# Spreading an mLSTM's running maxima by a DRAM round trip instead of matmuls, and the last layer norms in three VectorE steps: one change to a streaming encoder layer

## The chip, the cores and the metric

The kernel runs on one core of one Trainium2 chip. The metric is device time in microseconds for one execution of the whole layer; a figure for a kernel is the median of its runs. One execution was also recorded by the hardware profiler; its own time and its span (first to last instruction) are given beside the runs, since the views of the profile belong to that execution.

The core's engines each run their own instruction stream: PE (TensorE, with its weight loads listed apart as PEld), DVE (VectorE), ACT (ScalarE), POOL (GpSimd) and SP (SyncE, which only issues transfers here). DMA transfers are issued from an engine's queue and run beside the engines; SPq and POOLq are the queues of SP and GpSimd.

## The reference, cut to what matters

One layer of an encoder is computed for a prompt of 2048 tokens and a batch of 8 short samples of 16 tokens, model width 1024. Two groups of heads work on one input projection; their outputs are concatenated, projected, added to the input and normalised; a convolutional feed-forward block with its own norm follows.

```python
def trunk_layer(x, ...):
    qm, km, vm, om, ip, fp, qa, ka, va = split_in(x @ w_in)
    logi, logf = ip + b_igate, log_sigmoid(fp + b_fgate)
    hm, C1, n1, m1 = mlstm_chunkwise(qm, km * 128**-0.5, vm, logi, logf, C0, n0, m0)
    hm = sigmoid(om) * head_norm(hm, g_mlstm_norm)
    ha = sliding_window_attention(rope(qa), rope(ka), va)
    h = layer_norm(ALPHA * x + concat(hm, ha) @ w_out, ln1_g, ln1_b)
    f = conv_ffn(h, conv_prev, w_up, w_conv, b_conv, w_down)
    return layer_norm(ALPHA * h + f, ln2_g, ln2_b)

def layer_norm(x, g, b):
    return (x - mean(x)) * rsqrt(var(x) + 1e-5) * g + b
```

The mLSTM has 4 heads of 128. It goes through the prompt in chunks and carries a matrix memory `C`, a vector `n` and a stabiliser `m` per head:

```python
    def step(carry, inp):
        C, n, m = carry
        qc, kc, vc, li, lf = inp
        b = cumsum(lf)
        inter = b + m
        dmat = where(causal, b[:, None] - b[None, :] + li[None, :], -inf)
        mt = maximum(inter, max(dmat))
        w_inter = exp(inter - mt)
        s = (qc @ kc.T) * exp(dmat - mt[:, None])
        num = w_inter * (qc @ C) + s @ vc
        den = w_inter * (qc @ n) + sum(s)
        h = num / maximum(abs(den), exp(-mt))
        ...
```

Write `M` for the running maximum of `li - b` and the carried `m`, so that `mt = b + M`. Then `w_inter = exp(m - M)`, and the weight of source position s for query position l is `exp(li - b at s, minus M at l)`. The kernel works with `M` directly: it needs `M` of each query position along the free axis of a tile, the same on all 128 partitions.

## The kernel before

**Tiling.** Tokens come in 17 tiles of 128: 16 of the prompt (`NPT`) and one that holds the 8 x 16 sample tokens. The mLSTM takes a whole prompt tile of 128 as one chunk. All products of weights with tokens are done with three matmuls, each operand split in a high and a low part: `split` (L215) has ScalarE cast the high part (L217) and VectorE subtract it from the source (L218). Dense projections use a Strassen-like scheme of seven products per block.

**Stages.** By the trace: input projection until about 650 us (`i_product`, L688), output projection until about 890 (`group` and `o_block`, matmuls at L222 to L224, with the first norm, `norm`, L1548), a transition, up-projection from 935 to 1880 (matmuls at L1831), and down-projection until the end (`f_downs`, matmuls at L2034).

**How the recurrent work is woven in.** `Chains` (L157) holds three generators: the sample tile, the mLSTM of the prompt (`m_chain`, L1039) and the windowed attention (`a_chain`). While the input and output projections run, each dense piece of work adds its cost in ns to a clock, and a generator takes its next step once its due time has passed and enough of the five PSUM banks of the chains are expected to be free. A step says at its `yield` what it cost, after how long the next one is due and how many banks that one needs. These numbers only set the order in which instructions are written. TensorE keeps exactly that order (its schedule is manual, L230 and on); the instructions of the other engines are ordered by the framework's scheduler, each engine then runs its own list in order.

**One prompt tile of the mLSTM before.** `m_rows` (L1065) transposes the gates into rows of four heads by 128 positions, scans the cumulative sum `bc`, forms `a_` = li - b and scans the running maximum `M` (L1072), starting from the carry `self.mc`. `hilo` (L1004) splits `M` into two fp32r parts, `hl`. `y_row` writes -b - M into the rows 32 to 35 of `ay`, whose rows 0 to 3 hold `a_`. The next carry is b + M at the last position (L1076).

`m_tile` (L1175) then spreads `M` over the partitions on TensorE: `m_rep` (L1090) multiplies `hl` with a selector, one matmul per head, into the PSUM bank `pm`, which then holds -M on all partitions. `m_cols` (L1013) multiplies the broadcast carry with an identity (plain fp32, which appears as two matmuls) and transposes `ay`, both into `pcol`, and copies 40 columns to SBUF. VectorE adds the causal mask, giving `dt` (L1099); ScalarE makes `emt`, then four steps `wi` = exp(pm + carry) (L1111) and four steps exp(dt + a) (L1105). Next come the scores `qk @ k` and the transposed keys on TensorE, and VectorE's products `sd`, `kw` and `qk * wi` (L1192). Last come `pnum` (L1199 and the line behind it), which takes `sd` and the weighted `qk`, and the new memory `C`. In a tile's rhythm the load and `m_rows` of the next tile are written after the head norm of this one.

Two lines carry the spreading:

```python
self.nc.tensor.matmul(pm[:, h], self.sel[:, h:h + 1].to_broadcast([36, P]), self.hl[i], start=True, stop=True)
nc.tensor.matmul(ps[:, 0:4], mp.to_broadcast([MH, P]), self.ident[:MH, :MH], start=True, stop=True)
```

**GpSimd's other work in these stages** is a memset of the ones column of `v1` in `m_load` (L1079), and in each norm the power -1/2 of variance + eps, `lsc` (L1545), on one column.

**The down-projection.** `f_downs` goes through three blocks of tiles (`FBLOCKS`, 6, 6 and 5), in each through seven products and in each product through six units of the inner dimension. After the last unit of a product, `after` (L2037) empties its banks: for product 1 ScalarE copies one bank to another, the tile `fht` (L2041), which the matmuls of a later product go on adding to; for the others VectorE adds the bank to the sum `yacc` of a token tile. When a tile's sum is complete, `finish` (L2065) is appended to `pending`; in each unit the first two entries of `pending` advance by one step. `finish` runs `norm_steps` (L1561): the first step takes the statistics; the second computes -mean times `lsc` on VectorE (one column), the normalised tile on ScalarE (L1567), the product with g on VectorE (L1568) and the addition of b on GpSimd (L1569; on VectorE in the last block), and issues the transfer of the result from GpSimd's queue (from SP's in the last block). The last tiles of the last block go through `norm_last`, on VectorE and SP alone. `d_weights` (L1952) and `d_tokens` (L1970) run five and six units ahead: SP issues the weight load `wraw`, then `split` makes `uw` from it and `fu` from the tokens `r`.

Of the kernel before, what the change touches and what calls it, by code (L numbers as in the profile page):

```python
# [8 lines left out]
F32 = mybir.dt.float32  # L9
# [5 lines left out]
P = 128  # L15
# [8 lines left out]
MH = 4  # L24
# [180 lines left out]
class Prog:  # L205
# [89 lines left out]
    def setup(self):  # L295
# [14 lines left out]
        self.zw = [dp.tile([4, P, 1024], F32, name=f"zw{j}") for j in range(NFF)]  # L310
        self.zc = [dp.tile([P, 2, len(FBLOCKS[0]) * P], F32, name=f"zc{j}") for j in range(NFF)]
        self.zt = dp.tile([2, NK2, P, D], F32, name="zt")
        self.zf = [dp.tile([NFF, P, len(b) * P], F32, name=f"zf{i}") for i, b in enumerate(FBLOCKS)]
# [613 lines left out]
    def t_setup(self):  # L927
# [31 lines left out]
        nc.vector.memset(self.C, 0.0)  # L959
        self.mc = self.one("mc0", [MH, 1])  # L960
        nc.vector.memset(self.mc, 0.0)
# [32 lines left out]
    def row(self, nm, dt=F32):  # L994
        return self.work("r_" + nm, [MH, P], dt, 1 if nm == "b" else 2)

# [15 lines left out]

    def m_cols(self, i, mp=None):  # L1013

        nc = self.nc
        ps = self.bank([P, 40], "pcol")
        if mp is not None:
            nc.tensor.matmul(ps[:, 0:4], mp.to_broadcast([MH, P]), self.ident[:MH, :MH], start=True, stop=True)
        nc.tensor.transpose(ps[:, 4:40], self.ay[i], self.ident[:36, :36])
        c0 = 4 if mp is None else 0  # L1020
        col = self.work("col", [P, 40], bufs=2)
        nc.vector.tensor_copy(col[:, c0:], ps[:, c0:])
        return col

    def m_emt(self, col):
        emt = self.work("emt", [P, MH], bufs=2)
        self.nc.scalar.activation(emt, col[:, 36:40], AF.Exp)
        return emt
# [10 lines left out]
    def m_chain(self):  # L1039
# [4 lines left out]
        for t in range(NPT):  # L1044
# [3 lines left out]
            if pend is None:  # L1048
                pend = self.m_load(t, b, ti), *self.m_rows(t, b, ti)
                yield 300, 7000, 2  # L1050
            else:
                yield 0, 1000, 2
            hn = self.m_norm(*(yield from self.m_tile(t, *pend)))
# [11 lines left out]
    def m_rows(self, t, b, ti):  # L1065
        V = self.nc.vector
        lf, li = self.gate_rows(self.logs_of(b), ti)
        i = t % 2
        bc, a_, M = self.row("b"), self.ay[i][0:4], self.row("M")
        V.tensor_tensor_scan(bc, lf, self.seg[:, 0], 0.0, op0=ALU.add, op1=ALU.add)  # L1070
        V.tensor_sub(a_, li, bc)
        V.tensor_tensor_scan(M, self.seg[:, 0], a_, self.mc, op0=ALU.add, op1=ALU.max)  # L1072
        self.hilo(i, M)
        self.y_row(i, bc, M)
        mp, self.mc = self.mc, self.work("mc", [MH, 1], bufs=3)
        V.tensor_add(self.mc, bc[:, P - 1:P], M[:, P - 1:P])  # L1076
        return i, mp

# [17 lines left out]

    def m_masked(self, pm, mask):
        dt = self.work("dt", [P, MH, P])
        self.nc.vector.tensor_tensor(dt, pm, mask.rearrange("p (o m) -> p o m", o=1).to_broadcast([P, MH, P]), op=ALU.add)  # L1099
        return dt  # L1100

    def m_exps(self, dt, col):

        for h in range(MH):
            self.nc.scalar.activation(dt[:, h], dt[:, h], AF.Exp, bias=col[:, 4 + h:5 + h])  # L1105

    def m_inter(self, pm, col):

        wi = self.work("wi", [P, MH, P])
        for h in range(MH):  # L1110
            self.nc.scalar.activation(wi[:, h], pm[:, h], AF.Exp, bias=col[:, h:h + 1])  # L1111
        return wi

# [60 lines left out]

    def m_tile(self, t, load, i, mp):  # L1175
        nc = self.nc
        V = nc.vector
        qk, v1, og = load
        pm = self.m_rep(i)
        col = self.m_cols(i, mp)  # L1180
        dt = self.m_masked(pm, self.mcau)
        yield 600, 2800
        emt = self.m_emt(col)
        wi = self.m_inter(pm, col)
        self.m_exps(dt, col)
# [162 lines left out]
    def t_sample(self):  # L1348
# [8 lines left out]
        lf, li = self.gate_rows(self.logs_of(b), ti)  # L1357
        bc, M = [self.row(n) for n in ("b", "M")]
        ar = self.work("sd", [MH, P], name="ar")
# [8 lines left out]
        nc.sync.dma_start(a["m_s"], ms)  # L1368
        x = self.work("dt", [MH, P], name="x")

# [177 lines left out]
    def norm(self, y, g, bb, z):  # L1548
# [10 lines left out]
        self.nc.sync.dma_start(z, y)  # L1559

    def norm_steps(self, y, g, bb, adder=None):  # L1561
        nc = self.nc
        V = nc.vector
        mv, s = self.stats(y)
        yield
        V.scalar_tensor_tensor(s[:, 1:2], mv[:, 0:1], -1.0, s[:, 0:1], op0=ALU.mult, op1=ALU.mult)
        nc.scalar.activation(y, y, AF.Identity, bias=s[:, 1:2], scale=s[:, 0:1])  # L1567
        V.tensor_mul(y, y, g)  # L1568
        (adder or nc.gpsimd).tensor_add(y, y, bb)  # L1569

# [428 lines left out]
    def f_downs(self):  # L1999
# [65 lines left out]
        def finish(t, b, step):  # L2065
            if b == nb - 1 and step == 3:
                self.norm_last(ys[t], *ln2, a["y"][t], st if t == last_tile else None)
                return
            end = b == nb - 1
            yield from self.norm_steps(ys[t], *ln2, V if end else nc.gpsimd)  # L2070
            (nc.sync if end else nc.gpsimd).dma_start(a["y"][t], ys[t])

# [55 lines left out]
```

## Time and profile before

| | us |
|---|---|
| median of 3 runs | 2362.39 (2361.93 to 2363.34) |
| the profiled execution, its own time | 2366.53 |
| its span | 2364.8, granted TensorE clock 0.994 |

Busy time by stage in that execution, from a view of busy time in windows of the span:

| stage (us) | PE | DVE | ACT | POOL | DMA share | GB/s |
|---|---|---|---|---|---|---|
| 0 to 300, input projection | 287.6 | 210.7 | 133.7 | 15.0 | 0.83 | 286 |
| 300 to 650, input projection | 344.6 | 268.6 | 244.5 | 12.0 | 0.90 | 304 |
| 650 to 890, output projection | 240.0 | 202.7 | 149.5 | 24.8 | 0.69 | 231 |
| 935 to 1880, up-projection | 934.1 | 722.1 | 516.1 | 90.9 | 0.83 | 284 |
| 1880 to 2365, down-projection | 466.8 | 391.5 | 219.5 | 61.0 | 0.61 | 202 |

How the rows of the trace read. A row of the timeline gives the start in us from the span's start, the duration in us, the engine, the line of the kernel (L1072 is line 1072), the operation, out<-in by tile names with their shapes, and how many instructions are joined in it; brackets at its end give the engine's idle time ahead of it and what ended that. A row of the windows gives the stretch, its length, then busy time (and instructions) of PE, PEld, DVE, ACT and POOL, the granted clock (1.00 is full speed), the mean busy share of the 16 DMA engines, and GB/s. A row of the waits names an engine, the group that waited, the engine and tile that released it, and then total us, number and mean. A row of the DMA issues gives out<-in, the queue, how many, the size of each and the median us from issue to landing. A row of the groups gives after its count the total busy us and the mean ns of one, then the idle time ahead of it and what ended most of it.

### The profile page before, as it was taken

Reading aid. Unit: us, or ns where it says so; the run is one execution under the profiler, and the core shown is the slowest. Engines: PE = TensorE matmul, PEld = TensorE weight load, DVE = VectorE, ACT = ScalarE, POOL = GpSimd, SP = SyncE. Lnnn points to the kernel's source line nnn. Section 1 sums busy time; section 2 is a strip of 40 time slices with the busy share of each in tenths; the row PEclk is TensorE's granted clock in tenths of the full one; section 3 lists DMA queues with packets and bytes.
Section 4 is the critical chain, followed back from the end, with each engine's and each line's share of the span. In section 5 each row is a group of like instructions: output and inputs, shape, how many; then the busy total and the mean of one; then the engine's idle time right before and its main releaser. Section 6 shows DMA issues by size and latency. Waiting matters only on the chain.

```text
span 2364.8 us, 39830 instructions
## 1 busy us (share of the span) xinstructions
PE 2316.2 (98%) x14425; PEld 2122.7 (90%) x14425; DVE 1834.5 (78%) x3221; ACT 1284.3 (54%) x2423; POOL 209.4 (9%) x281
## 2 busy tenths in 40 slices
PE   8999999999999999999999999999999999999998
PEld 7999999899987777999999999999999978778776
DVE  8676587797688888987888676777766786895987
ACT  5453366777766565555556455555544544544543
POOL 0001000000000112200000000002000100400400
PEclk9999999999999999999999999999999999999999
DMA  7888889889976657887777889878988776657653
GB/s 279 283 302 286 288 287 324 276 291 318 314 264 227 225 204 248 286 306 289 274 270 257 307 316 314 308 242 297 315 275 260 212 284 219 232 170 219 228 166 107
DMA packets 296933, 624.98 MB, mean 264 GB/s; under 512 B 47004, under 2 KB 140192, under 8 KB 296736
## 3 DMA queue, kind: packets, MB, share of 16 engines
q1 hardware_dynamic: 294144, 612.99, 76.3%
q0 software_dynamic: 1728, 6.29, 0.7%
q10 hardware_dynamic: 864, 3.15, 0.3%
q8 instruction: 114, 1.87, 0.3%
q14 instruction: 83, 0.68, 0.1%
HBM read 451.78 MB, written 170.56 MB: 263 GB/s over the span
## 4 chain that ended last, share of the span: by engine, by line
PE 69%; DVE 7%; DMA 3%; issue 2%; ACT 1%; POOL 1%; SPq 0%; DVEq 0%; POOLq 0%; ACTq 0%
PE dps L1831 18%; PE fup L1831 18%; PE fht L2034 5%; PE dps L700 5%; PE dps L2034 5%; PE fup L2034 3%; PE dps L222 2%; PE dps L224 2%; PE dps L223 2%; PE ppo L1337 1%; DVE uw L218 1%; PE ppt L1331 1%; PE psc L1288 1%; DVE hl L218 1%; DMA yacc<-zh 1%
## 5 line engine op out<-in xcount | busy, mean ns | idle before, releaser
L1831 PE MATMUL dps<-hh,uw 128*128 128x384 f32 (+1 forms) x1848 | 481.5, 329 | 6.7 <-ACT u L1856 1.9
L1831 PE MATMUL fup<-hh,uw 128*128 128x384 f32 (+1 forms) x1848 | 480.1, 328 | 2.5 <-ACT u L1856 2.1
L1831 PEld LDWEIGHTS dps<-hh,uw 128*128 128x128 f32 x1848 | 330.0, 188 | 10.3 <-ACT u L1856 2.9
L1879 DVE SCALAR_TENSOR_TENSOR cc<-u,cw,cc 128x768 f32<-128x768 f32 (+1 forms) x264 | 252.4, 977 | 106.2 <-ACT cc L1877 104.3
L1831 PEld LDWEIGHTS fup<-hh,uw 128*128 128x128 f32 x1848 | 330.1, 188 | 3.6 <-ACT u L1856 2.9
L1831 PE MATMUL fup<-hl,uw 128*128 128x384 f32 (+1 forms) x924 | 302.9, 328 | 1.7 <-DVE hl L218 1.7
L1831 PE MATMUL dps<-hl,uw 128*128 128x384 f32 (+1 forms) x924 | 302.5, 327 | 0.0
L700 PE MATMUL dps<-w,oh 128*128 128x256 f32 x1344 | 258.7, 287 | 2.6 <-DVE zev L773 1.1
L217 ACT CAST w<-wraw 128x1024 fp32r<-128x1024 f32 (+2 forms) x167 | 163.0, 984 | 141.4 <-PE dps L700 67.8
L218 DVE TENSOR_TENSOR w<-wraw,w 128x1024 fp32r<-128x1024 f32 (+2 forms) x167 | 189.1, 1139 | 56.2 <-ACT w L217 53.6
L217 ACT CAST uw<-wraw 128x1024 fp32r<-128x1024 f32 x126 | 122.9, 978 | 196.8 <-PE dps L2034 99.3
L700 PEld LDWEIGHTS dps<-w,oh 128*128 128x128 f32 x1344 | 213.4, 190 | 14.6 <-issue 8.9
L218 DVE TENSOR_TENSOR uw<-wraw,uw 128x1024 fp32r<-128x1024 f32 x126 | 150.7, 1198 | 63.4 <-ACT uw L217 63.1
L1877 ACT ACTIVATE cc<-u,cw 128x768 f32<-128x768 f32 (+1 forms) x132 | 129.6, 997 | 118.0 <-DVE u L1870 60.2
L700 PE MATMUL dps<-w,ol 128*128 128x256 f32 x672 | 189.2, 282 | 0.0
L2034 PE MATMUL fup<-uw,fu 128*128 128x512 f32 x726 | 178.2, 401 | 9.5 <-ACT fht L2041 6.9
L2034 PEld LDWEIGHTS fup<-uw,fu 128*128 128x128 f32 x726 | 138.1, 191 | 45.0 <-ACT fht L2041 7.8
L700 PE MATMUL dps<-oh,w 128*128 128x256 f32 x896 | 167.1, 282 | 10.0 <-ACT zev L759 3.7
L1831 PEld LDWEIGHTS fup<-hl,uw 128*128 128x128 f32 x924 | 173.5, 188 | 2.5 <-DVE hl L218 2.5
L1831 PEld LDWEIGHTS dps<-hl,uw 128*128 128x128 f32 x924 | 173.5, 188 | 0.0
L2034 PE MATMUL dps<-uw,fu 128*128 128x512 f32 x660 | 165.0, 395 | 0.0
L700 PEld LDWEIGHTS dps<-oh,w 128*128 128x128 f32 x896 | 139.7, 188 | 16.1 <-issue 4.1
(326 smaller groups left out, 4596.2 us busy)
## 6 DMA issues: line engine op xcount, KB each, us to landing
uw<-zw SPq DMA_DIRECT2D x176, 512.0 KB, 4.6
zw<-uw SPq DMA_DIRECT2D x88, 512.0 KB, 3.1
w<-zws SPq DMA_DIRECT2D x72, 512.0 KB, 6.3
wv<-wup SPq DMA_DIRECT2D x66, 512.0 KB, 5.5
wraw<-wi SPq DMA_DIRECT2D x65, 512.0 KB, 4.7
wraw<-zt SPq DMA_DIRECT2D x60, 512.0 KB, 4.2
wraw<-wdn SPq DMA_DIRECT2D x45, 512.0 KB, 4.1
wraw<-wo SPq DMA_DIRECT2D x40, 512.0 KB, 4.6
```

The lines of the kernel that those rows point to most:

```text
L217: nc.scalar.copy(hi, src)
L218: nc.vector.tensor_sub(lo, src, hi.bitcast(F32))
L222: mm(out, ah, bh, start=start, stop=False)
L223: mm(out, ah, bl, start=False, stop=False)
L224: mm(out, al, bh, start=False, stop=stop)
L700: mm(o, l, r, start=s in (1, 7) and c == k == i == 0, stop=k == 3 and i == 2, skip_group_check=True)
L1288: nc.tensor.matmul(ps[kvh][:, j, :nk], q[rs, j0 + j], k[rs, sel], start=i == 0, stop=i == 2)
L1331: nc.tensor.transpose(pp[:, j * P:(j + 1) * P], scs[j // 2][:, 2 * kvh + j % 2, kt * P:(kt + 1) * P], self.ident)
L1831: mm(ps, l[:, k], r[:, k], start=s in (1, 7) and k == 0 and i == 0, stop=k == 3 and i == 2, skip_group_check=True)
L1877: S.activation(c[:, v], u[:, v, 2:2 + n], AF.Identity, bias=w[3], scale=w[2])
L1879: V.scalar_tensor_tensor(c[:, v], u[:, v, i:i + n], w[i], c[:, v], op0=ALU.mult, op1=ALU.add)
L2034: mm(ps, l[:, k, c], r[:, k], start=s in (1, 4, 7) and u == 0 and k == 0 and i == 0, stop=u == nu - 1 and k == n - 1 and i == 2, skip_grou ...
```

## The change

Two parts that do not touch each other.

**The maxima.** The tile of `M` becomes four rows of 129: 128 maxima and, in the last column, the carry the scan starts from. `m_rows` no longer splits it. It issues, on GpSimd's queue, a transfer of these rows to a small DRAM tile `zM` (two of them, used in turn), and behind it, on the same queue, a transfer that reads the 516 numbers back to every one of 128 partitions, into the SBUF tile `wi` (one buffer). The read waits for the write to land. `m_cols` keeps only the transpose of `ay`; `m_rep` is called for the sample tile alone. `dt` is now the mask minus `wi`, read from SBUF; `m_inter` overwrites `wi` in place with exp(-wi + its last column). The next carry is written into the last column of the next tile's rows. The costs and banks that `m_chain` and `m_tile` declare are lowered to match (two banks become one, 600 ns become 200). In the sample tile two scratch rows move into one work tile.

**The last norms.** `norm_steps` is gone. `finish` takes the statistics in its first step, computes (y - mean) * g in one VectorE instruction in the second, and y * lsc + b in one VectorE instruction in the third, with the transfer of the result behind it, from the same queues as before.

```diff
@@ -309,6 +309,7 @@
+        self.zM = [dp.tile([1, MH, P + 1], F32, name=f"zM{i}") for i in range(2)]
@@ -957,7 +958,9 @@
-        self.mc = self.one("mc0", [MH, 1])
+
+        self.M = self.row("M")
+        self.mc = self.M[:, P:]
         nc.vector.memset(self.mc, 0.0)
@@ -992,7 +995,7 @@
     def row(self, nm, dt=F32):
-        return self.work("r_" + nm, [MH, P], dt, 1 if nm == "b" else 2)
+        return self.work("r_" + nm, [MH, P + (nm == "M")], dt, 1 if nm == "b" else 2)
@@ -1010,21 +1013,18 @@
-    def m_cols(self, i, mp=None):
+    def m_cols(self, i):
         nc = self.nc
-        ps = self.bank([P, 40], "pcol")
-        if mp is not None:
-            nc.tensor.matmul(ps[:, 0:4], mp.to_broadcast([MH, P]), self.ident[:MH, :MH], start=True, stop=True)
-        nc.tensor.transpose(ps[:, 4:40], self.ay[i], self.ident[:36, :36])
-        c0 = 4 if mp is None else 0
-        col = self.work("col", [P, 40], bufs=2)
-        nc.vector.tensor_copy(col[:, c0:], ps[:, c0:])
+        ps = self.bank([P, 36], "pcol")
+        nc.tensor.transpose(ps, self.ay[i], self.ident[:36, :36])
+        col = self.work("col", [P, 36], bufs=2)
+        nc.vector.tensor_copy(col, ps)
         return col
@@ -1047,9 +1047,9 @@
                 pend = self.m_load(t, b, ti), *self.m_rows(t, b, ti)
-                yield 300, 7000, 2
+                yield 300, 7000, 1
             else:
-                yield 0, 1000, 2
+                yield 0, 1000, 1
@@ -1066,15 +1066,18 @@
-        bc, a_, M = self.row("b"), self.ay[i][0:4], self.row("M")
+        bc, a_, M = self.row("b"), self.ay[i][0:4], self.M[:, :P]
         V.tensor_tensor_scan(bc, lf, self.seg[:, 0], 0.0, op0=ALU.add, op1=ALU.add)
         V.tensor_sub(a_, li, bc)
         V.tensor_tensor_scan(M, self.seg[:, 0], a_, self.mc, op0=ALU.add, op1=ALU.max)
-        self.hilo(i, M)
+        self.nc.gpsimd.dma_start(self.zM[i][0], self.M)
+        wi = self.work("wi", [P, MH, P + 1])
+        self.nc.gpsimd.dma_start(wi.rearrange("p h m -> p (h m)"), self.zM[i].rearrange("o h m -> o (h m)").to_broadcast([P, MH * (P + 1)]))
         self.y_row(i, bc, M)
-        mp, self.mc = self.mc, self.work("mc", [MH, 1], bufs=3)
+        self.M = self.row("M")
+        self.mc = self.M[:, P:]
         V.tensor_add(self.mc, bc[:, P - 1:P], M[:, P - 1:P])
-        return i, mp
+        return i, wi
@@ -1094,22 +1097,25 @@
-    def m_masked(self, pm, mask):
+    def m_masked(self, pm, mask, minus=False):
         dt = self.work("dt", [P, MH, P])
-        self.nc.vector.tensor_tensor(dt, pm, mask.rearrange("p (o m) -> p o m", o=1).to_broadcast([P, MH, P]), op=ALU.add)
+        mask = mask.rearrange("p (o m) -> p o m", o=1).to_broadcast([P, MH, P])
+        if minus:
+            self.nc.vector.tensor_sub(dt, mask, pm)
+        else:
+            self.nc.vector.tensor_add(dt, pm, mask)
         return dt
-    def m_inter(self, pm, col):
-
-        wi = self.work("wi", [P, MH, P])
+    def m_inter(self, wi):
+
         for h in range(MH):
-            self.nc.scalar.activation(wi[:, h], pm[:, h], AF.Exp, bias=col[:, h:h + 1])
-        return wi
+            self.nc.scalar.activation(wi[:, h, :P], wi[:, h, :P], AF.Exp, bias=wi[:, h, P:], scale=-1.0)
+        return wi[:, :, :P]
@@ -1172,16 +1178,15 @@
-    def m_tile(self, t, load, i, mp):
+    def m_tile(self, t, load, i, wi):
         qk, v1, og = load
-        pm = self.m_rep(i)
-        col = self.m_cols(i, mp)
-        dt = self.m_masked(pm, self.mcau)
-        yield 600, 2800
+        col = self.m_cols(i)
+        dt = self.m_masked(wi[:, :, :P], self.mcau, True)
+        yield 200, 2800
         emt = self.m_emt(col)
-        wi = self.m_inter(pm, col)
+        wi = self.m_inter(wi)
         self.m_exps(dt, col)
@@ -1558,16 +1563,6 @@
-    def norm_steps(self, y, g, bb, adder=None):
-        nc = self.nc
-        V = nc.vector
-        mv, s = self.stats(y)
-        yield
-        V.scalar_tensor_tensor(s[:, 1:2], mv[:, 0:1], -1.0, s[:, 0:1], op0=ALU.mult, op1=ALU.mult)
-        nc.scalar.activation(y, y, AF.Identity, bias=s[:, 1:2], scale=s[:, 0:1])
-        V.tensor_mul(y, y, g)
-        (adder or nc.gpsimd).tensor_add(y, y, bb)
@@ -2066,9 +2061,13 @@
-            end = b == nb - 1
-            yield from self.norm_steps(ys[t], *ln2, V if end else nc.gpsimd)
-            (nc.sync if end else nc.gpsimd).dma_start(a["y"][t], ys[t])
+            y, (g, bb) = ys[t], ln2
+            mv, sc = self.stats(y)
+            yield
+            V.scalar_tensor_tensor(y, y, mv[:, 0:1], g, op0=ALU.subtract, op1=ALU.mult)
+            yield
+            V.scalar_tensor_tensor(y, y, sc[:, 0:1], bb, op0=ALU.mult, op1=ALU.add)
+            (nc.sync if b == nb - 1 else nc.gpsimd).dma_start(a["y"][t], y)
```

More of the change, by code (lines that the diff above doesn't have):

```diff
@@ L1026, in m_emt @@
         emt = self.work("emt", [P, MH], bufs=2)
-        self.nc.scalar.activation(emt, col[:, 36:40], AF.Exp)
+        self.nc.scalar.activation(emt, col[:, 32:36], AF.Exp)
         return emt
@@ L1104, in m_exps @@
         for h in range(MH):
-            self.nc.scalar.activation(dt[:, h], dt[:, h], AF.Exp, bias=col[:, 4 + h:5 + h])
-    def m_inter(self, pm, col):
-        wi = self.work("wi", [P, MH, P])
+            self.nc.scalar.activation(dt[:, h], dt[:, h], AF.Exp, bias=col[:, h:h + 1])
+    def m_inter(self, wi):
         for h in range(MH):
-            self.nc.scalar.activation(wi[:, h], pm[:, h], AF.Exp, bias=col[:, h:h + 1])
-        return wi
+            self.nc.scalar.activation(wi[:, h, :P], wi[:, h, :P], AF.Exp, bias=wi[:, h, P:], scale=-1.0)
+        return wi[:, :, :P]
     def m_scores(self, qk):
@@ L1357, in t_sample @@
         lf, li = self.gate_rows(self.logs_of(b), ti)
-        bc, M = [self.row(n) for n in ("b", "M")]
+        bc, M = self.row("b"), self.work("dt", [MH, 2, P], name="Mx")
+        M, x = M[:, 0], M[:, 1]
         ar = self.work("sd", [MH, P], name="ar")
@@ L1368, in t_sample @@
         nc.sync.dma_start(a["m_s"], ms)
-        x = self.work("dt", [MH, P], name="x")
         b3 = lambda r: r.rearrange("p (b l) -> p b l", b=DB)
```

## The prediction, as it was put on record before the run

> **What bounds the kernel now.** I read the head of the page first, then busy time by stage, then what TensorE itself waited for.
>
> ```profile
> span 2364.8 us, 39830 instructions
> PE 2316.2 (98%) x14425; PEld 2122.7 (90%) x14425; DVE 1834.5 (78%) x3221; ACT 1284.3 (54%) x2423; POOL 209.4 (9%) x281
> ```
>
> ```profile
> 430.00:650.00 220.00, 219.41 (x1828) 203.42 (x1828) 169.37 (x499) 160.54 (x411) 7.90 (x12) 1.00 0.90 300
> ...
> 720.00:800.00 80.00, 80.00 (x457) 63.28 (x456) 69.98 (x200) 51.83 (x145) 8.07 (x8) 1.00 0.67 225
> ```
>
> The columns are PE, PEld, DVE, ACT, POOL, granted clock, DMA share and GB/s. The first stretch lies in the input projection, the second in the output projection; the recurrent chain of the 16 prompt tiles is woven into both. TensorE is busy 219.4 of 220 and 80.0 of 80 us at full clock. So in these stages an instruction taken off TensorE is time off the end, as long as nothing it waits for comes later. The second thing to see is VectorE: 77% busy in the first stretch, 87% in the second. That is the engine on which a new wait would have to be absorbed.
>
> In the down-projection TensorE stops at one place that bears on the change, once behind each of two block boundaries:
>
> ```profile
> PE fup L2034 <- ACT fht L2041: 6.9, 2, 3.5
> ```
>
> **Part one: what TensorE no longer does.** Each prompt tile spreads the running maxima by four matmuls (`pm`) and the carry by one plain fp32 matmul, which shows as two (`pcol<-ident,mc`). One tile on TensorE:
>
> ```profile
> 817.08 0.66 PE L1094 MATMUL pm<-hl,sel 36*128 36x128 f32 x4
> 817.67 0.38 PE L1018 MATMUL pcol<-ident,mc 4*128 4x4 f32 x2
> 817.98 0.25 PE L1019 MATMUL pcol<-ident,ay 36*128 36x36 f32 x1
> 818.16 1.08 PE L1337 MATMUL ppo<-pth,kva 128*64 128x512 f32 x4
> ```
>
> From the start of `pm` to the start of the transpose that stays is 817.98 - 817.08 = 0.90 us. Sixteen tiles make 14.4 us. That is the ceiling; the floor is nothing, if TensorE waits for as long afterwards. In the built order the other matmuls of a tile keep their distances (27 and 21 projection matmuls between the `pcol` transpose, the scores and `pnum` in the output projection, 54 and 42 in the input projection), so I count no other gain or loss on TensorE's own side. A PSUM bank per tile is freed too, worth nothing while TensorE waits for no bank.
>
> **Part two: the round trip that takes its place.** After the scan of the maxima GpSimd writes a row of 4 x 129 to DRAM, waits for it to land, and reads it back to 128 partitions, 264 KB. VectorE's `dt` is the first to wait for it. No such transfer stands in this trace, so its time C, from the scan's end to the landing, comes from the nearest rows:
>
> ```profile
> zh<-ymix SPq DMA_DIRECT2D x17, 512.0 KB, 3.0
> ...
> y<-yacc POOLq DMA_DIRECT2D x12, 512.0 KB, 4.3
> ...
> v<-zv SPq DMA_DIRECT2D x17, 256.0 KB, 7.3
> ...
> lnp<-ln_g SPq DMA_DIRECT2D x2, 256.0 KB, 4.8
> ...
> conv_p<-prev SPq DMA_DIRECT2D x1, 44.0 KB, 1.7
> ```
>
> The same 512 KB written to DRAM take 3.0 us from SP's queue and 4.3 from GpSimd's: 1.3 us for that queue. A small write then takes 1.7 + 1.3 = 3.0. The read resembles `lnp`, a row spread over the partitions from DRAM: 4.8 + 1.3 = 6.1. So C = 9.1 us. From below it is two transfers at the small row's 1.7, 3.4 us; from above 4.3 for the write and 7.3 + 1.3 for the read, 12.9. I take 9.1, because `lnp` is the same kind of read.
>
> The Trainium skill, "DMA: Bandwidth & Descriptors", section "Latency and other measured facts", puts a DMA's fixed cost at about 2 us, most of it the round trip to memory. By it C would be an estimated 5 us, and the sum below would lose its 5 us of waits; the rows here, 3.0 to 7.3 us under load, speak for more.
>
> What C does is seen in two tiles. One of the output projection:
>
> ```profile
> 811.91 0.47 DVE L1072 TENSOR_TENSOR_SCAN r_M<-k_seg,mc,ay 4x128 f32<-4x128 f32 x1
> ...
> 812.88 0.20 DVE L1007 CAST hl<-r_M 4x128 fp32r<-4x128 f32 x1
> ...
> 813.33 0.27 DVE L1008 TENSOR_TENSOR hl<-r_M,hl 4x128 fp32r<-4x128 f32 x1
> ...
> 816.50 0.69 DVE L1608 SCALAR_TENSOR_TENSOR ymix<-ymix,dps 128x512 f32<-128x512 f32 x1 [2.54 <-PE dps L224]
> ...
> 818.08 0.64 DVE L1099 TENSOR_TENSOR dt<-pm,k_mcau 128x512 f32<-128x512 f32 x1
> ...
> 825.87 1.23 DVE L893 TENSOR_TENSOR ol<-xraw,oh 128x1024 fp32r<-128x1024 f32 x1 [2.23 <-ACT oh L892]
> ...
> 830.99 0.68 DVE L1192 TENSOR_TENSOR qk<-qk,wi 128x512 f32<-128x512 f32 x1
> ```
>
> ```profile
> 833.96 0.38 PE L1199 MATMUL pnum<-v,sd 128*128 128x129 f32 x2
> ```
>
> Now `dt` starts 5.7 us after the scan ends at 812.4, and the last operand of `pnum`, `qk`, is ready at 831.7, 19.3 us after the scan. In these VectorE is idle 2.5 + 2.2, so it works 14.6; the two `hl` steps that go are 0.47 of it, which leaves 14.1. The built order of the changed kernel has 3.8 us of VectorE work between scan and `dt`, so 10.3 lie behind. With C = 9.1, `qk` is ready at 812.4 + 9.1 + 10.3 = 831.8. TensorE comes to `pnum` at 833.96 - 0.90 = 833.1. No wait, 1.3 us to spare.
>
> One of the input projection:
>
> ```profile
> 564.97 0.47 DVE L1072 TENSOR_TENSOR_SCAN r_M<-k_seg,mc,ay 4x128 f32<-4x128 f32 x1
> ...
> 576.66 0.42 DVE L1292 CUSTOM_DVE_ANT_0 sc<-psc,k_mswa 128x256 f32<-128x256 f32 x1 [1.48 <-PE psc L1288]
> ...
> 580.56 0.16 DVE L1306 TENSOR_TENSOR asm<-asm,aes 128x4 f32<-128x4 f32 x1 [2.04 <-ACT sc L1303]
> ...
> 586.77 0.68 DVE L1192 TENSOR_TENSOR qk<-qk,wi 128x512 f32<-128x512 f32 x1
> ```
>
> ```profile
> 589.71 0.38 PE L1199 MATMUL pnum<-v,sd 128*128 128x129 f32 x2
> ```
>
> Scan's end 565.4, `qk` ready 587.5: 22.1 us, of them 3.5 idle, so 18.6 of work, 18.1 without `hl`. The built order puts only 2.9 before `dt`, 15.2 behind: `qk` ready at 565.4 + 9.1 + 15.2 = 589.7, TensorE there at 588.8. A wait of 0.9 us, less whatever idle time still absorbs. Over all tiles I take 0.3 us each, 16 x 0.3 = +5 us; between 0 and 0.9 x 16 = 14 at this C.
>
> Queued behind the waiting instructions: on VectorE everything after `dt`, weight splits and PSUM evictions among it, is already in the 10.3 and 15.2. On GpSimd the memset of `v1` and the small powers of the norms stand behind the read, which waits some 3 us for the write. Their users on VectorE come mostly behind `dt` and so wait no longer than it does; without that cover it would be up to 3 us in each of the seven tiles of the output projection, 21 us. The reads add 16 x 264 KB = 4.2 MB, at 300 GB/s 14 us of transfer over some 580 us, which lifts the DMA share of 0.90 by about 0.03. I count it at nothing; SP's queue issues the same transfers as before, some in another order. ScalarE's four `wi` steps read SBUF in place of PSUM: nothing to the path.
>
> **Part three: the norms of the down-projection.** Removed per tile are a tiny VectorE step, ScalarE's pass and GpSimd's addition; VectorE gets two fused steps in two visits. This is the place where TensorE stops now:
>
> ```profile
> 2063.14 2.44 POOL L1569 TENSOR_TENSOR yacc<-yacc,f_ln_b 128x1024 f32<-128x1024 f32 x1
> 2063.24 0.20 DVE L1543 BATCH_NORM_AGGREGATE lmv<-lst 128x2 f32<-128x12 f32 x1
> 2063.36 3.03 DVE L218 TENSOR_TENSOR fu<-r,fu 128x768 fp32r<-128x768 f32 x1
> ```
>
> ```profile
> 2063.39 0.37 SPq L1966 DMA_DIRECT2D wraw<-wdn  x1
> ...
> 2068.24 1.24 ACT L1567 ACTIVATE yacc<-yacc,lsc 128x1024 f32<-128x1024 f32 x1 [5.18 <-DVE lsc L1566]
> 2069.38 1.03 ACT L217 CAST uw<-wraw 128x1024 fp32r<-128x1024 f32 x1
> 2070.32 0.58 ACT L2041 COPY fht<-fup 128x512 f32<-128x512 f32 x1
> ```
>
> ```profile
> 2070.95 4.34 PE L2034 MATMUL fup<-uw,fu 128*128 128x512 f32 x11 [3.47 <-ACT fht L2041]
> ```
>
> VectorE's split of `fu` stretches to 3.03 us while GpSimd adds; the scale `lsc` comes late, ScalarE stands 5.2 us before its norm pass, and the copy `fht`, which TensorE needs, stands behind it. With the pass gone, late next is the cast of `uw`, which waits for a weight load issued at 2063.39. By the page that load takes:
>
> ```profile
> wraw<-wdn SPq DMA_DIRECT2D x45, 512.0 KB, 4.1
> ```
>
> It lands at 2067.5, the cast ends 1.0 later, the copy at 2069.1; TensorE, which stopped at 2070.95 - 3.47 = 2067.5, waits 1.6 in place of 3.5. So 1.9 us come back, twice: -3.7. The bounds are 0, if the load slips, and -6.9. VectorE's side:
>
> ```profile
> L1558 DVE SCALAR_TENSOR_TENSOR ymix<-ymix,lsc,o_ln_b 128x1024 f32<-128x1024 f32 x15 | 19.1, 1273 | 1.2 <-POOL lsc L1545 1.2
> ```
>
> Two such steps are 2.5 us, against a product of about 1.2 and a stretch of about 2 us (3.03 now for a split), so VectorE comes out even. Results leave GpSimd's queue in the visit after the one that wrote them; the next block's `yacc` needs them no sooner. In the last block the two tiles finish one visit later, hidden under the last products.
>
> **Sum.** -14.4 + 5 - 3.7 = -13.1 us. The profiled execution took 2366.5 us (span 2364.8), so 2353.4 by it; the runs' median, 2362.4, lies 4.1 lower, so **2349 us**.
>
> **Rivals.** *Quick round trip* (C below about 8): no tile waits, and `fht` is not held: -14.4 - 6.9 = -21.3, 2341 us. Two transfers at the small row's 1.7 us would make it so; the loaded rows of 4.3 and 4.8 us speak against. The figure of the Trainium skill's section named above would make it so too. *Saving eaten* (C of 10 to 11): up to 1.3 us beyond 9.1 only tiles like the second pay, 8 x 1.5 = 12 us, and the sum is about -1: 2361. TensorE's work is gone but comes back as waits at `pnum`. *Slower*: C of 12 us, near the upper rows. VectorE stands at `dt` for it, and TensorE at `pnum` behind: 8 x 2.9 + 8 x 1.6 = 36 us over C = 9.1, so +23: 2385. It decides from C = 10.7 on. For it: VectorE is 87% busy in the output projection and GpSimd's queue is in order; against: VectorE idles 31 to 51 us in stretches of 230 us in which it can catch up.
>
> **How the numbers follow.** Forecast 0.45, quick 0.25, eaten 0.13, slower 0.17. The likeliest alone spans 2343 to 2356 (waits 0 to 14 us, norms 0 to -6.9, not both at their ends). The range reaches down past the quick case and up past the eaten one: 2339 to 2365, with the slower case left out. About 0.2%, 4.7 us, is what a measurement here tells from no change. Forecast and quick lie beyond it: faster 0.70; same 0.13; slower 0.17.
>
> **What would show it.** `dt` should start 8 to 10 us after the scan's end, and waits of TensorE at `pnum` should total under 10 us; both projections together should end 8 to 14 us earlier. Splits during the norms should last about 1 us and never 3, and the wait for `fht` should be under 2 us each. The forecast is wrong if VectorE's idle time before `dt` passes 6 us per tile, or if another eviction takes the place of `pnum`.

## The result, and the profile after

The changed kernel takes **2402.4 us** (2401.7 to 2407.6) against 2362.2 before: ratio 1.0175, 95% interval 1.0157 to 1.0193. The forecast was 2349 in a range of 2339 to 2365. Both the direction and the size were wrong; the rival called "slower" had the direction and priced it at 2385.

First the head of the page of the changed kernel, to be laid beside that of the kernel before.

```profile
span 2399.9 us, 39622 instructions
...
PE 2317.9 (97%) x14329; PEld 2121.0 (88%) x14329; DVE 1817.2 (76%) x3187; ACT 1266.7 (53%) x2409; POOL 195.1 (8%) x301
```

TensorE has 96 matmuls fewer and is busy for 1.7 us longer. So the stages have to be taken apart. The same view of windows, cut where the trace shows the last matmul of each stage: of the kernel before,

```profile
294.00:649.80 355.80, 350.42 (x2906) 326.56 (x2906) 272.86 (x800) 245.96 (x632) 11.97 (x18) 0.99 0.90 301
649.80:933.70 283.90, 282.03 (x1567) 221.93 (x1566) 240.54 (x632) 170.68 (x427) 30.50 (x27) 1.00 0.69 234
...
1879.00:2364.80 485.80, 467.77 (x1989) 373.92 (x1987) 392.37 (x494) 219.54 (x273) 62.04 (x43) 0.99 0.61 201
```

and of the changed kernel:

```profile
294.00:691.70 397.70, 357.32 (x2862) 328.27 (x2862) 267.68 (x798) 248.98 (x651) 23.72 (x38) 0.96 0.84 277
691.70:978.00 286.30, 279.20 (x1507) 218.59 (x1506) 234.49 (x598) 165.44 (x409) 37.46 (x39) 0.99 0.70 234
...
1925.50:2399.90 474.40, 463.94 (x1990) 371.93 (x1988) 383.18 (x492) 203.39 (x259) 29.18 (x31) 0.99 0.62 206
```

More than the whole loss is in the first row, the input projection from its first prompt tile on: +41.9 us. The output projection loses 2.4, the up-projection between these rows 2.2, the down-projection gains 11.4; together that is the 35.1 us between the two spans. In the first row TensorE's idle time goes from 5.4 to 40.4 us (length less busy time), +35.0, and its busy time rises by 6.9 although work was taken away: the granted clock falls from 0.99 to 0.96, and 4% of 397.7 is 15.9 us against 1% of 355.8, 3.6. These shares are rounded and count idle time too; over the time in which TensorE works, the clock of the two traces costs 12.4 and 3.2 us.

What TensorE waited for in this stretch of the changed kernel, from the view of waits (total us, times, and then the longest wait, not the mean):

```profile
PE dps L701 <- ACT dps L796: 9.1, 3, 6.9
PE ppo L1342 <- ACT pth L1337: 4.9, 1, 4.9
PE dps L701 <- ACT zev L768: 4.7, 3, 2.9
PE dps L701 <- ACT zev L760: 3.6, 3, 1.8
...
PE pnum L1205 <- DVE qk L1197: 1.0, 2, 0.7
```

Not `pnum`, where the prediction looked: there the waits of both projections come to 5.0 us, no more than it forecast. Of some 40 us here, 28.9 are at the projection's own matmuls (`dps`), 20.5 of them for ScalarE to empty a PSUM bank and 7.2 for VectorE to do so. Why ScalarE is late stands in the timeline of the second prompt tile of the changed kernel:

```profile
341.44 0.47 DVE L1072 TENSOR_TENSOR_SCAN r_M<-k_seg,r_M,ay 4x128 f32<-4x128 f32 x1
...
342.19 0.58 POOL L1073 DMA_DIRECT2D zM<-r_M  x1 [2.05 <-DVE r_M L1072]
...
347.51 0.57 POOL L1075 DMA_DIRECT2D wi<-zM  x1 [4.74 <-ACT zev L760]
...
354.55 0.69 DVE L1104 TENSOR_TENSOR dt<-k_mcau,wi 128x512 f32<-128x512 f32 x1 [9.05 <-DMA wi<-zM]
...
355.27 0.40 ACT L1117 ACTIVATE wi<-wi 128x128 f32<-128x128 f32 x1 [8.11 <-DVE dt L1104]
355.58 0.58 ACT L796 COPY dps<-dps 128x512 f32<-128x512 f32 x1
...
356.21 0.58 PE L701 MATMUL dps<-oh,w 128*128 128x256 f32 x1 [6.85 <-ACT dps L796]
```

The scan ends at 341.9, the read lands just before 354.55. VectorE stands 9.05 us at `dt`. ScalarE stands 8.11 us at the first `wi` step, which overwrites what `dt` reads and so waits for `dt` to end, up to 0.69 us longer than for the read alone; no run gives it a tile of its own. The copy of a projection bank (L796) is next in ScalarE's order, and TensorE stands 6.85 us for it. Over the whole run these waits of the two engines come to:

```profile
ACT wi L1117 <- DVE dt L1104: 83.1, 15, 8.8
...
DVE dt L1104 <- DMA wi<-zM: 76.1, 15, 9.1
```

Then the clock, in windows over the second tile's moment:

```profile
350.00:353.00 3.00, 0.00 (x0) 0.00 (x0) 0.00 (x0) 0.00 (x0) 0.00 (x0) 1.00 1.01 359
353.00:356.00 3.00, 0.00 (x0) 0.00 (x0) 1.45 (x2) 0.73 (x2) 0.00 (x0) 0.53 0.41 142
356.00:359.00 3.00, 2.79 (x12) 2.63 (x12) 2.97 (x14) 2.18 (x9) 0.00 (x0) 0.50 0.52 152
359.00:362.00 3.00, 3.00 (x26) 2.79 (x26) 2.40 (x7) 3.00 (x10) 0.00 (x0) 0.83 0.32 113
```

When TensorE starts again it is granted half its clock, then 0.83: 12 matmuls in 3 us, then 26. At 0.50 and 0.83 the two busy windows lose 1.4 and 0.5 us, on top of the 6.85. The Trainium skill, "TensorE: Matmul & The Clock Gate", Part 1, has the clock halve after about 3.4 us without work and come back after as long a busy time. The trace agrees: TensorE stops at 349.4, and 0.53 in the second window puts the half clock at about 353.2; it starts again at 356.2, and 0.83 in the last puts the full clock at about 360.0. That is 3.8 us each time.

### The profile page after: what moved, and what is told of

It reads as the page before. It is cut to its first block, busy times and chain, and to the rows that moved or that the text cites. A ratio compares the mean times of both kernels' runs of the same rounds, so it can differ in the third digit from the quotient of the medians.

```text
span 2399.9 us, 39622 instructions
## 1 busy us (share of the span) xinstructions
PE 2317.9 (97%) x14329; PEld 2121.0 (88%) x14329; DVE 1817.2 (76%) x3187; ACT 1266.7 (53%) x2409; POOL 195.1 (8%) x301
## 4 chain that ended last, share of the span: by engine, by line
PE 56%; DVE 7%; DMA 5%; ACT 2%; issue 2%; POOL 0%; SPq 0%; DVEq 0%; ACTq 0%; POOLq 0%
PE dps L1826 18%; PE fup L1826 17%; PE dps L2029 6%; PE fup L2029 6%; PE fht L2029 6%; DMA wi<-zM 1%; PE dps L222 1%; DVE hl L218 1%; PE dps L224 1%; PE dps L223 1%; DVE uw L218 1%; DVE w L218 1%; DMA hst<-zh 0%; DVE sc L1297 0%; DVE ymix L1561 0%
## 5 line engine op out<-in xcount | busy, mean ns | idle before, releaser
L1826 PEld LDWEIGHTS dps<-hh,uw 128*128 128x128 f32 x1848 | 330.0, 188 | 10.7 <-ACT u L1851 2.7
L701 PE MATMUL dps<-w,oh 128*128 128x256 f32 x1344 | 263.9, 290 | 13.8 <-ACT zev L757 3.1
L218 DVE TENSOR_TENSOR uw<-wraw,uw 128x1024 fp32r<-128x1024 f32 x126 | 142.3, 1131 | 65.0 <-ACT uw L217 64.8
```

The costliest lines, as they stand in the source:

```text
L218: nc.vector.tensor_sub(lo, src, hi.bitcast(F32))
L701: mm(o, l, r, start=s in (1, 7) and c == k == i == 0, stop=k == 3 and i == 2, skip_group_check=True)
L1826: mm(ps, l[:, k], r[:, k], start=s in (1, 7) and k == 0 and i == 0, stop=k == 3 and i == 2, skip_group_check=True)
```

## The experiments

Theory **L**: the length of the trip costs, because VectorE and ScalarE stand in order at `dt` and `wi`. Theory **Q**: the transfers themselves, or GpSimd's queue. Theory **W**: the new weave. The table has medians, ratios to the runs before on the same chip with their intervals, the total of VectorE's waits at `dt` by the view of waits, and stage lengths from the traces (last matmul to last matmul, the transition counted with the output projection; the first from 294 us on; the last to the span's end). A stage length is that of one execution, and executions of the kernel before lie between 2357 and 2368 us, so some us in a single stage carry little. The medians of the kernel before beside the runs lie between 2362.2 and 2364.4, so a difference between two rows is good to about 2 us.

| kernel | us | ratio | at `dt` | input | output | down |
|---|---|---|---|---|---|---|
| before | 2362.2 | | 9.6 | 355.9 | 283.8 | 486.6 |
| after | 2402.4 | 1.0175 [1.0157, 1.0193] | 76.1 | 397.8 | 286.2 | 475.2 |
| norms_only | 2350.4 | 0.9938 [0.9923, 0.9953] | 9.4 | 351.7 | 281.8 | 475.1 |
| maxima_only | 2415.2 | 1.0215 [1.0200, 1.0231] | 80.5 | 398.6 | 287.0 | 486.0 |
| weave_only | 2375.8 | 1.0049 [1.0034, 1.0064] | 13.8 | 365.8 | 285.9 | 486.5 |
| unread_trip | 2366.8 | 1.0022 [1.0010, 1.0034] | 9.3 | 355.7 | 282.3 | 486.4 |
| double_trip | 2438.1 | 1.0319 [1.0299, 1.0338] | 116.7 | 417.5 | 303.0 | 476.3 |
| queue_sync | 2356.4 | 0.9970 [0.9960, 0.9980] | 30.1 | 364.5 | 275.0 | 475.2 |
| sync_write | 2380.2 | 1.0078 [1.0060, 1.0095] | 65.1 | 385.8 | 283.5 | 475.2 |
| old_weave | 2390.1 | 1.0120 [1.0103, 1.0137] | 72.4 | 384.5 | 286.0 | 475.2 |
| sync_old_weave | 2340.6 | 0.9906 [0.9892, 0.9921] | 24.0 | 349.1 | 276.0 | 475.2 |
| hidden_trip | 2367.9 | 1.0013 [1.0004, 1.0023] | 3.8 | 364.9 | 285.1 | 475.7 |
| hidden_same_rows | 2358.1 | 0.9973 [0.9964, 0.9983] | 0 | 363.5 | 275.7 | 475.2 |
| sync_covered | 2355.4 | 0.9970 [0.9961, 0.9979] | 0.9 | 364.0 | 278.0 | 476.4 |
| sync_double | 2365.2 | 1.0002 [0.9989, 1.0015] | 32.8 | 363.4 | 288.5 | 475.2 |

### The parts apart

norms_only is the kernel before with the new `finish`, maxima_only the changed kernel with `norm_steps` put back.

> Only the new norms of the down-projection, the maxima as before. Between the two traces the down-projection shrank from 485.8 to 474.4 us. If the two parts are independent, this kernel is 11 us faster than before: 2351 us. If the step of the prediction were right in size, -3.7: 2358. If the shorter down-projection only came of the later start or other order of transfers, no change: 2362.

> Only the round trip of the maxima, the norms as before. The input projection grew by 41.9 us and the output projection by 2.4 between the traces. Independent parts: 2362 + 40 + 11 = 2413 us. If the parts interact, anything below 2405.

The parts add: -12.8 us (2363.2 for the kernel before beside it) and +52.0 make +39.2, and the change is +40.2.

### The new weave, and a trip that nobody waits for

```diff
-                yield 300, 7000, 2
+                yield 300, 7000, 1
-                yield 0, 1000, 2
+                yield 0, 1000, 1
-        yield 600, 2800
+        yield 200, 2800
```

> The kernel before with the costs and banks that the change declares (one bank in place of two, 200 ns in place of 600), so its steps fall at other places among the projection's matmuls; no round trip. Theory L (the latency of the round trip, during which VectorE and ScalarE stand in order): within 5 us of 2362. Theory W (the other weave alone brings the waits at the projection's banks): 2385 or more.

```diff
+        self.nc.gpsimd.dma_start(self.zM[i][0], M)
+        wx = self.work("sd", [P, MH, P], name="wx")
+        self.nc.gpsimd.dma_start(wx.rearrange("p h m -> p (h m)"), self.zM[i].rearrange("o h m -> o (h m)").to_broadcast([P, MH * P]))
```

> The kernel before with the write and the broadcast read of the maxima added on GpSimd's queue; the read lands in the tile that later takes the weighted scores, and nothing reads it, so dt and wi wait for TensorE's copy as before. Theory L: 2362 to 2368 us. Theory Q (the transfers' share of the DMA engines, or GpSimd's queue standing behind the read): 2385 or more. In the trace the time from the scan's end to the landing should again be near 10.7 us.

Between the theories' lines for the weave: +12.5 us with no trip at all. So a part of the loss is W. The unread trip, on GpSimd's queue and with nearly as many bytes, costs 3.6 us, with the lists of TensorE, VectorE and ScalarE in the input projection in the order of the kernel before; Q is not the cause of the loss. Its read lands later than the old `dt` starts in 13 of 16 tiles, and no compute step waits for it.

### The trip longer, and covered

double_trip sends the row through a second DRAM tile (`zN`, then `zM`) on the same queue. hidden_same_rows lets the rows' VectorE steps go first and writes `dt` a step later in a fixed place; hidden_trip also issues the rows a step earlier.

```diff
+        with self.tc.high_priority():
+            return self.m_rows(t, b, ti)
...
         col = self.m_cols(i)
-        dt = self.m_masked(wi[:, :, :P], self.mcau, True)
         yield 200, 2800
+        dt = self.m_masked(wi[:, :, :P], self.mcau, True)
...
+            self.tc.keep_in_program_order(self.nc.vector.tensor_sub(dt, mask, pm))
```

> The changed kernel with one more transfer of 2 KB from DRAM to DRAM on GpSimd's queue between the write and the read, so the trip lasts some 5 us longer per tile and moves hardly more bytes. Theory L: the 5 us are stood out at dt on VectorE in nearly all of 16 tiles, +50 to +80: 2450 to 2480 us. Theory Q by bytes: within 5 us of 2402.

> The changed kernel with the round trip covered: the rows of the next tile are issued right behind the head norm instead of one step later, their VectorE steps go first, and dt is written one step later and keeps that place on VectorE. By the built order VectorE has 10 to 20 us of work between the scan and dt, where the changed kernel has 3.5 to 8. Theory L (the latency is what costs): VectorE's idle time at dt falls from 76 us in all to under 15, and the time to 2340 to 2360, that is at or below the kernel with the new norms alone (2350). Theory Q (transfers and GpSimd's queue): stays above 2385.

> As hidden_trip, but the rows are issued at the step where the changed kernel issues them; 8 to 14 us of VectorE work between scan and dt. Theory L: about half of the idle time at dt stays, 2360 to 2375.

double_trip is 35.7 us slower than the changed kernel, for 40.6 us more at `dt`: less than the 50 to 80 expected, since the scan-to-`dt` time grew by 3.7 us in the median (10.8 to 14.5), not by 5. Covering the trip gives 34 to 44 us back, as L has it, and Q's "above 2385" falls. Both forecasts missed, though. hidden_same_rows leaves no idle time at `dt`, where half was expected, and at 2358.1 lies below its range. hidden_trip ends at 2367.9, above its range, with waits at other matmuls:

```profile
PE ppt L1341 <- ACT pth L1342: 4.3, 2, 3.1
PE ppt L1341 <- ACT sc L1319: 3.7, 2, 3.1
PE dps L701 <- ACT dps L796: 3.6, 3, 2.1
PE pht L1180 <- DVE ql L218: 3.0, 1, 3.0
```

That a `dt` moved back makes the steps behind it late would fit these waits, but hidden_same_rows moves it as well and loses less: 9.4 of the 9.8 us between the two lie in the output projection (285.1 against 275.7). What the earlier rows cost there is open.

### The queue

queue_sync issues both transfers from SP (`nc.sync.dma_start`), sync_write the write alone.

> The changed kernel with write and read issued from SP's queue instead of GpSimd's. If GpSimd's queue is what makes the trip long (1.3 us per transfer in the prediction), the trip falls from 10.7 to about 8 us and the time to 2385 or less. If the transfers are as long from SP's queue, the loads behind them on SP stand 5 us per tile as well, and the time rises above 2410.

> The changed kernel with the write alone on SP's queue, the broadcast read stays on GpSimd's. In queue_sync the read was issued 2 to 4 us after the scan in place of 4 to 7, and took as long as before. If the write's leg is what GpSimd's queue made long: dt starts 8 to 9 us after the scan and the time is 2356 to 2370. If the read's leg was: dt stays at 10 to 11 us and the time near 2400.

From SP's queue the median read is issued 3.1 us after the scan's end instead of 5.3, and `dt` starts at 8.0 instead of 10.8. VectorE's waits at `dt` fall by 46.0 us and the time by 46.0. That the two are equal is luck: TensorE's list is the same in both kernels, but with the queue the framework also moved some 80 of VectorE's 1132 instructions in the input projection and some 60 of ScalarE's 863, and no run separates that from the shorter trip. The same tile as above, in queue_sync:

```profile
341.21 0.47 DVE L1072 TENSOR_TENSOR_SCAN r_M<-k_seg,r_M,ay 4x128 f32<-4x128 f32 x1
...
341.71 0.27 SPq L1073 DMA_DIRECT2D zM<-r_M  x1
...
344.01 0.32 SPq L1075 DMA_DIRECT2D wi<-zM  x1
...
349.67 0.69 DVE L1104 TENSOR_TENSOR dt<-k_mcau,wi 128x512 f32<-128x512 f32 x1 [4.40 <-DMA wi<-zM]
```

sync_write lies between, with `dt` at 9.7 and 2380: each leg is worth about half.

### Old weave with the trip; a longer trip on SP's queue

old_weave and sync_old_weave take the three `yield` figures back (the diff above, reversed). sync_covered is sync_old_weave with hidden_same_rows' edits, sync_double sync_old_weave with double_trip's `zN`, all on SP.

> The changed kernel with the costs and banks of the kernel before (two banks, 600 ns), so the steps of the chain fall nearer to their old places; the round trip stays on GpSimd's queue. weave_only lost 12.5 us by the new figures alone. If that adds to the rest: 2402 - 12 = 2390 us. If the stalls at dt swallow it (places that matter without stalls don't matter with them): 2402.

> queue_sync (2356 us) with the costs and banks of the kernel before. If the weave's 12 us add: 2344. If not: 2356.

> Trip on SP's queue, old costs and banks, rows' VectorE steps first and dt written one step later in a fixed place. If VectorE's idle time at dt (30 us in queue_sync) is all that is left of the latency: 2335 to 2342, which is TensorE's 14 us and the norms' 13 below the kernel before. If the later dt makes scores and pnum late instead: 2350 or more.

> sync_old_weave (2341 us, 24 us idle at dt) with a third transfer of 2 KB from DRAM to DRAM between write and read, all on SP's queue. If what costs is the trip's length past some 25 us of idle time at dt in all, whichever queue it is on: the time rises by as much as the idle time at dt does, 20 to 50 us. If it was GpSimd's queue in itself: within 5 us of 2341.

The weave's loss comes off in both, 12.3 and 15.8 us. **sync_old_weave, at 2340.6 us, beats both kernels.** sync_covered misses: no idle time at `dt`, yet the input projection is 15 us longer than sync_old_weave's. That the later `dt` makes its users late, the second case of its forecast, fits TensorE's waits there for `sd` and `qk` (4.2 us by the view of waits), but no run takes this apart. sync_double is 24.6 us slower than sync_old_weave, with `dt` at 11.3 us instead of 7.2. So a longer trip costs on SP's queue too; but the idle time at `dt` rose by 8.8 us only, and not by as much as the time: the built order has more VectorE work ahead of `dt`, 6.3 us in the median tile instead of 4.6. ScalarE shows more of it. Its waits at `wi` for `dt` rose by 30.7 us, from 17.2 to 47.9; in old_weave they are 79.6. Over these three kernels the time rises by 0.8 us for each us that ScalarE stands at `wi`.

### Which figure of the weave; which half of the norms

> The kernel before with one bank declared in place of two at the two steps of m_chain, the cost of 600 ns kept. weave_only, with both, lost 12.5 us. If the banks are the cause (steps are written before a bank is free): 2370 to 2376. If the cost figure is: 2362.

> The kernel before with 200 ns declared in place of 600 in m_tile, the two banks kept. If the cost figure is the cause of the 12.5 us: 2370 to 2376. If the banks are: 2362.

weave_banks: 2367.2, ratio 1.0012 [1.0001, 1.0022], +2.8 us. weave_cost: 2373.3, ratio 1.0038 [1.0023, 1.0053], +9.0. The declared cost is most of it: 200 for 600 puts the chain's steps at other matmuls of the projection, with TensorE's work unchanged. Where that costs time is clear in weave_only alone, whose input projection is 9.9 us longer (in an execution 5 us over its median), with waits of TensorE of 10.6 us in place of 5.4. In weave_cost's trace no stage grows by more than 2 us (1.0 in the input projection, 1.9 in the output).

norms_add_dve keeps the old two steps but has VectorE add b; norms_add_pool is norms_only with the third step cut into a VectorE scaling and GpSimd's addition.

> The kernel before, its norms in the old two steps with ScalarE's pass kept; only the addition of b goes from GpSimd to VectorE in all blocks. If GpSimd's addition is what made lsc late and stretched VectorE's splits: near norms_only, 2350 to 2354. If ScalarE's pass in front of fht is what costs: 2358 to 2363.

> norms_only with its third step cut in two: VectorE scales by lsc, GpSimd adds b (the last block as in norms_only). ScalarE has no pass. If ScalarE's pass is what costs: 2350 to 2354. If GpSimd's addition does, by itself: 2358 to 2364, with splits of fu stretched to 3 us as before.

norms_add_dve: 2352.2, ratio 0.9948 [0.9932, 0.9965], so -12.2 us by moving the addition alone. norms_add_pool: 2358.2, 0.9974 [0.9965, 0.9983], -6.2: without ScalarE's pass, but with GpSimd's addition, half comes back. TensorE's waits for `fht` (6.9 us before) are 0.4 us in norms_add_dve and nothing in norms_add_pool, where two others take their place:

```profile
PE fup L2024 <- DVE yacc L2051: 2.5, 1, 2.5
PE fht L2024 <- DVE yacc L2053: 2.4, 1, 2.4
```

The group of VectorE's token splits, in norms_only, norms_add_dve and norms_add_pool in this order (count, then total us and mean ns):

```profile
L218 DVE TENSOR_TENSOR fu<-r,fu 128x768 fp32r<-128x768 f32 (+2 forms) x132 | 106.6, 814 | 5.9 <-ACT fu L217 5.4
```

```profile
L218 DVE TENSOR_TENSOR fu<-r,fu 128x768 fp32r<-128x768 f32 (+2 forms) x132 | 106.8, 816 | 5.4 <-ACT fu L217 5.0
```

```profile
L218 DVE TENSOR_TENSOR fu<-r,fu 128x768 fp32r<-128x768 f32 (+2 forms) x132 | 117.5, 896 | 5.4 <-ACT fu L217 5.1
```

Where GpSimd adds, these splits are 11 us longer in all, and 13 in the kernel before (119.9).

## Why the prediction was wrong, point by point

**TensorE's 14.4 us: right.** In sync_old_weave the two projections are 6.8 and 7.8 us shorter than before, 14.6 together. So close a match is luck: each trace is one execution, and 24.0 us of idle time at `dt` are still in it.

**"I count no other gain or loss on TensorE's own side": failed.** The distances between a tile's own matmuls were looked at, but not where the whole chain lands among the projection's matmuls. weave_only: +12.5.

**C = 9.1: mis-sized.** The median from scan to `dt` was 10.8. The rows of the changed kernel:

```profile
wi<-zM POOLq DMA_DIRECT2D x16, 258.0 KB, 5.6
...
zM<-r_M POOLq DMA_DIRECT2D x16, 2.0 KB, 4.2
```

The read, set at 6.1, took 5.6. The write, set at 3.0, took 4.2: a small row of 1.7 us was no measure for it, 512 KB from the same queue had taken 4.3. The remaining 1.0 us (10.8 less these two), for getting the write and then the read issued, had no term in the sum.

**"Over all tiles I take 0.3 us each", at `pnum`: failed, and it is the step that turned the sign.** The weave and the norms make +12.5 - 12.8, TensorE's work -14.4; to come to +40.2 the trip's waits must be 54.9 us, if the parts add, and not 5. Three things were left out. ScalarE stands behind `dt` as well: "ScalarE's four `wi` steps read SBUF in place of PSUM: nothing to the path" overlooked that they now wait for the trip and have the projection's bank copies behind them. The operands were followed only to `pnum`, where TensorE did wait just 5.0 us, and not to the banks of the projection, which were emptied late. And a stop of TensorE costs its clock as well, 9.2 us more in the input projection. Both signs that the prediction named for being wrong came: VectorE's idle time at `dt` passes 6 us in five of 16 tiles (4.8 in the mean, 9.1 at most), and other evictions took the place of `pnum`.

**The slower rival** had the right place on VectorE, but let the loss decide from C = 10.7 on, at 36 us over 2.9 us of C, or 12 per us. The loss starts sooner: with `dt` at 9.7 and 9.8 us, sync_write and old_weave already take 2380 and 2390. Nor is the price one number: between old_weave and sync_old_weave, with `dt` at 9.8 and 7.2 us, lie 49.5 us, or 19 per us; between double_trip and the changed kernel 10.

**The norms: place right, size wrong.** -3.7 was forecast, -12.8 measured. The stay of 1.6 us per boundary rested on a weight load issued at 2063.39. But that load was itself late: by the view of waits of SP's queue its issue stood 6.7 us for VectorE's split of an earlier weight, which ends at 2063.32. That split took 2.25 us beside GpSimd's addition, the next one 1.21 without it:

```profile
2061.07 2.25 DVE L218 TENSOR_TENSOR uw<-wraw,uw 128x1024 fp32r<-128x1024 f32 x1
...
2066.38 1.21 DVE L218 TENSOR_TENSOR uw<-wraw,uw 128x1024 fp32r<-128x1024 f32 x1
```

How much of the 6.7 us comes from the addition is not taken apart. With it off GpSimd the wait for `fht` is gone (6.9 us), which was the bound; in norms_add_dve that holds even with ScalarE's pass kept, so the pass held `fht` only because GpSimd's addition had made it late. The rest is the clock after each stop, in windows of the kernel before:

```profile
2070.90:2073.00 2.10, 2.06 (x7) 1.63 (x8) 2.10 (x3) 2.10 (x4) 1.57 (x1) 0.72 1.02 371
2073.00:2076.00 3.00, 3.00 (x10) 2.38 (x9) 3.00 (x2) 1.01 (x2) 2.05 (x2) 0.63 0.31 121
```

At 0.72 and 0.63 some 1.7 us are lost behind a stop of 3.5, 3.4 for the two. That makes 10.3 of the 11.5 us by which the stage is shorter.

## What to carry to other kernels

A wait put on an in-order engine is paid by whatever stands behind it there, so follow every engine that takes it over, ScalarE here as much as VectorE, to the first PSUM bank that is emptied late, not only along the chain of operands. A trip through DRAM between two dependent steps wants the shortest queue: 2.6 us more per tile, with the order that the framework built around them, went with 2390 instead of 2341 us. And declared costs that only place work are a change of their own: alter them in a separate step.

## What the runs showed of the hardware

A write of 2 KB from GpSimd's queue took 4.2 us to land, hardly less than 512 KB in the kernel before (4.3). The whole trip with its 4.2 MB of reads cost only 3.6 us in unread_trip, where no compute step waits for its landing, although the DMA engines were busy 0.90 of the time in the input projection before.

Two stops of TensorE of 3.5 us cost a further 1.7 us each through the granted clock, one of 6.9 us a further 1.9.

GpSimd's addition of 128x1024 beside VectorE's splits of two SBUF operands lengthens those (3.03 us for one that takes 0.95 without it). The Trainium skill, "SBUF — State Buffer", section "SBUF: two separate sides", gives the two engines a shared pair of ports that one of them holds for a whole instruction; the 3.03 us agree with that, and no run here shows the lock itself.
